# Two hybrid blocks on one core: the input transposed once and used unnormalised by the first four projections, the attention mask written into PSUM by VectorE

## The chip, the cores and the metric

The kernel runs on one core of a Trainium2 chip. The metric is the device time of one execution in microseconds (us). The kernel before takes 1582.7 us, the median of three runs (1582.47 to 1582.87).

## The reference, cut to what matters

One sequence of 512 positions and 1024 features passes through two blocks. Everything is float32. The parts that the change touches:

```
h = concat(16 meta tokens, x)                      # 528 rows are used
n = h * rsqrt(mean(h*h, features) + 1e-6) * norm_mix_w
z = n @ w_in[1024, 7168]                           # q, k, v, glu (2 x 1024), two gates
s = (q * 64**-0.5) @ k.T                           # 8 heads x 2 maps, chunks of 64 positions
p = softmax(where(chunk(key) <= chunk(query), s, -1e30))
o = (p[0] - lam * p[1]) @ v;  y_att = rms(o) * subln_w * 0.2
u = glu[:1024] * sigmoid(glu[1024:]);  u = causal depthwise conv over 31 positions
u = silu(layernorm(u));  m = gate * y_att + gate * (u @ w_conv_out);  h = h + m @ w_out
... feed-forward with a 3 tap convolution, then block 2: an mLSTM, a linear recurrence,
    a 256-of-512 sparse attention with 4 heads, another feed-forward ...
```

The rms norm of a row is one factor per position. A projection of h * norm_mix_w therefore equals the projection of n once each of its columns (positions) is multiplied by that factor.

## The kernel before, in words

Activations lie with features on the 128 partitions: a tile holds 128 features by 528 positions, and eight tiles make the residual (`res`) or the normalised input (`xn`). Products are made with float32r parts. Each operand is split into a rounded part and the rest, and a product is three matmuls (weight high with activation high, weight high with activation low, weight low with activation high). A weight block of 1024 x 128 arrives by DMA as `raw`, ScalarE rounds it into `wh`, VectorE subtracts it into `wl`; three such pairs are buffered. A step (`step`, L566) is the six matmuls of one of the eight feature tiles, a projection (`units`, `one`) is eight steps.

Order is made at build time. `Build` keeps a model clock for TensorE (`pe`), and a model time for VectorE and for ScalarE (`Lane`, L158). Generators (`start`, `tick`) emit side work between the projection's steps when the model says that what they read is ready, and the operations of the 31 tap convolution wait in a list (`bg`) and are emitted one by one while the model's VectorE is no further than 0.3 us ahead of its TensorE. The hardware then runs each engine's instructions strictly in the order emitted. In `tick` the weight feed comes first, the convolution last.

The input phase (`load_x`, L601): five row tiles `xt` arrive by DMA. ScalarE squares them with a sum, the inverse roots are found in two parts (first two tiles, then three), VectorE multiplies the row tiles by the root into `xs`, and TensorE transposes `xs` into PSUM tile by tile (`parts`, `turn`), where ScalarE and VectorE make the two parts of `xn`. The raw tiles `xt` are transposed too, for the residual: four feature tiles into PSUM in `prepare`, the last rows and the four other feature tiles later in `raw`, which `block1_mix` starts. The projections start when `xn[0]` is there.

The list `units1` sets the order of projections in block 1: for each of eight feature tiles a pair of gated-unit projections (`glu`: `e_b` is the tanh half, `e_a` the value half) followed by three head projections (q, k, v, gate of a head in turn), then the remaining heads and gates. `glu(0)` runs its two projections in a skewed manner, as the input arrives. After the last value half the convolution has to run dry (`after_conv`), then `layer_norm` makes `us[0..7]`, and the projection with `w_conv_out` waits for each `us[k]`.

In `attention`, each head computes scores of four blocks of 128 queries. A mask is added by one small bfloat16 matmul per map and block (`ind` by `neg`, L331 to L336, L795 and L815). VectorE finds the row maximum, multiplies it by -0.125, and ScalarE does the exponential with scale 0.125. At the end of a head VectorE scales the four output blocks in one operation. The convolution (`conv_ops`, L753) of one feature tile is two `tensor_scalar`, 29 `scalar_tensor_tensor` that go in turn to two accumulators `a` and `b`, the sum of the two, and an add to `csum`.

Of the kernel before, what the change touches and what calls it, by code (L numbers as in the profile page):

```python
# [9 lines left out]
F32R = mybir.dt.float32r  # L10
# [7 lines left out]
P = 128  # L18
# [144 lines left out]
class Build:  # L163
# [159 lines left out]
    def constants(self):  # L323
        nc, c = self.nc, self.const
        self.ident = c.tile([P, P], F32, name="ident")
        make_identity(nc, self.ident)
        self.identb = c.tile([P, P], BF, name="identb")
        nc.vector.tensor_copy(self.identb, self.ident)
        self.ones = c.tile([P, P], F32, name="ones")
        nc.vector.memset(self.ones, 1.0)  # L330
        self.ind = c.tile([P, P], BF, name="ind")  # L331
        nc.vector.memset(self.ind, 0.0)
        for m in range(2):
            nc.vector.memset(self.ind[64 * m : 64 * m + 1, 0:64], 1.0)
        self.neg = c.tile([P, 64], BF, name="neg")
        nc.vector.memset(self.neg, NEG)  # L336
# [264 lines left out]
    def load_x(self):  # L601
        nc, io, V, S = self.nc, self.io, self.V, self.S
        x, meta = io["x"][0], io["meta_tokens"]
        self.res = [self.resp.tile([P, NT], F32, name=f"res{j}", tag="res") for j in range(KD)]
        self.xn = [None] * KD
        rows = [P, P, P, P, NMETA]
        xt = [self.flat(D) for _ in range(5)]
        xs = [self.flat(D) for _ in range(5)]
        v = self.sm(5, "xv")
        V.memset(v, 1.0)  # L610
        at = (1, 2, 3, 4, 0)
# [3 lines left out]
        for t in range(4):  # L615
# [15 lines left out]
        def turn(src, pt, j):  # L631
            for t in range(5):
                w = rows[t]
                self.tr(pt[:, t * P : t * P + w], src[t][:w, j * P : (j + 1) * P])

        def scale(ts, r, g):
            c = slice(512 * g, 512 * g + 512)
            for i, t in enumerate(ts):
                V.tensor_scalar(xs[t][: rows[t], c], xt[t][: rows[t], c], r[: rows[t], i : i + 1], None, op0=MUL)

        def inverse(lo, n):
            vb = v[:, lo : lo + n]
            yield self.due(vb)
            V.tensor_scalar(vb, vb, 1.0 / D, 1e-6, op0=MUL, op1=ADD)
            return (yield from self.rsqrt_act(vb, n))

        raws = [self.mm_ps(), self.mm_ps()]
        rawv = lambda j: raws[j // 2][:, (j % 2) * 512 : (j % 2) * 512 + 512]

        def square(t):  # L650
            S.activation(xs[t][: rows[t]], xt[t][: rows[t]], AF.Square, accum_out=v[: rows[t], at[t] : at[t] + 1])

        def prepare():

            S.activation(self.sm(1, "yw"), v[:, 0:1], AF.Sqrt)
            self.tr(raws[1][:, 0:8], w8[0:8])
            yield self.due(raws[1])
            V.tensor_copy(wmix, raws[1][:, 0:8])
            square(4)
# [9 lines left out]
            r = yield from inverse(2, 3)  # L669
            scale((1, 2, 3), r, 0)  # L670
            self.wp_max = 1
            for p in range(2):
                self.start(parts(p))
            yield self.due(raws[0])
            for j in range(2):
                S.activation(self.res[j][:, 0:512], rawv(j), AF.Copy)
            yield self.due(xs[3][:, 0:512])
            yield 4.0
            scale((1, 2, 3), r, 1)
            for j in range(2, 4):  # L680
                S.activation(self.res[j][:, 0:512], rawv(j), AF.Copy)

        def parts(p):

            for j in range(p, KD, 2):
                i, pt = yield from self.at_get()
                yield self.due(*[xs[t][: rows[t], j * P : (j + 1) * P] for t in range(5)])
                turn(xs, pt, j)
# [6 lines left out]
                yield self.due(n)  # L695
                self.at_put(i)

        def raw():
            i, pr = yield from self.at_get()
            for j in range(4):  # L700
                self.tr(pr[:, j * NMETA : (j + 1) * NMETA], xt[4][:NMETA, j * P : (j + 1) * P])
            yield self.due(pr)
            for j in range(4):
                S.activation(self.res[j][:, 512:], pr[:, j * NMETA : (j + 1) * NMETA], AF.Copy)
            self.at_put(i)
            for j in range(4, KD):
                yield 2.0
                i, pr = yield from self.at_get()
                turn(xt, pr, j)
                yield self.due(pr)  # L710
                S.activation(self.res[j], pr[:, :NT], AF.Copy)
                self.at_put(i)
# [3 lines left out]
        self.until(lambda: self.xn[0] is not None)  # L716
        return raw

    def one(self, segs, acts, evac):
# [4 lines left out]
        self.units([[(pt[:, o : o + m], m, c) for o, m, c in segs]], acts, evac=lambda u: evac(pt[:, lo : lo + n]))  # L724
# [28 lines left out]
    def conv_ops(self, j, u, a, b, csum):  # L753
        V = self.V
        w = lambda k: self.col("conv_dw_w", k * 8 + j)
        ops = [
            lambda: V.tensor_scalar(a, u[:, 0:NQ], w(0), self.col("conv_dw_b", j), op0=MUL, op1=ADD),
            lambda: V.tensor_scalar(b, u[:, 1 : 1 + NQ], w(1), None, op0=MUL),
        ]
# [10 lines left out]
    def attention(self, tp, h, qk, vs, ctx):  # L770
# [5 lines left out]
        made, used = [], [0]  # L776
        mask = lambda m: (self.ind[64 * m : 64 * m + 64, :], self.neg[64 * m : 64 * m + 64, :])
# [3 lines left out]
        def softmax(i):  # L781
            L = 144 + 128 * i
            q = lambda m: qT[64 * m : 64 * m + 64, 2 + 128 * i : 130 + 128 * i]
            mx, nb, l = self.sm(2, "mx"), self.sm(2, "nb"), self.sm(2, "ll")
            e = self.slot()

            def ex(m, sv):
                S.activation(e[:, m, :L], sv, AF.Exp, bias=nb[:, m : m + 1], scale=0.125, accum_out=l[:, m : m + 1])

            yield self.due(qT)  # L790
            if i < 3:
                i_at, pt = yield from self.at_get()
                for m in range(2):
                    mm(pt[:, 512 * m : 512 * m + L], q(m), k(m, 0, L), True, False)
                for m in range(2):  # L795
                    mm(pt[:, 512 * m + L - 64 : 512 * m + L], *mask(m), False, True)
                    if i == 0:
# [6 lines left out]
                V.tensor_reduce(mx, pair(pt)[:, :, :L], axis=AX.X, op=MAX)  # L804
                V.tensor_scalar(nb, mx, -0.125, None, op0=MUL)
# [1396 lines left out]
```

## Time and profile before

| what | value |
|---|---|
| median of three runs | 1582.7 us |
| the profiled execution's own time | 1582.17 us |
| its span, first to last instruction | 1580.4 us |
| TensorE busy | 1561.0 us, 99% of the span |
| VectorE busy | 1116.5 us, 71% |
| ScalarE busy | 650.8 us, 41% |

The span is the time from the first to the last instruction; the own time is 1.8 us more. A line of the profile's views names an engine (PE is TensorE, PEld its weight loads, DVE is VectorE, ACT is ScalarE), the line of the kernel, the operation, and the tiles written and read; L158 is the helper through which VectorE and ScalarE are called, L314 that of matmuls, L320 that of transposes, so a row is told by its tiles. `act<-u,par,act` is a tap of the long convolution, `at` and `mm` are PSUM tiles.

### The profile page before, as it was taken

The page shows a single profiled execution, that of the slowest core. Times are in us where ns is not written, and L with a number is a line of the kernel's source. Part 1 is how long each engine was busy: PE and PEld are TensorE (multiplying, and loading weights), DVE is VectorE, ACT ScalarE, POOL GpSimd, SP SyncE. Part 2 cuts the span into 40 slices and gives each one's busy share as a digit, 9 for nine tenths or more (in the row PEclk, how much of TensorE's full clock was granted, in tenths as well). Part 3 has the DMA queues.
Part 4 walks back from the last instruction along what each step waited for, and adds up shares of the span by engine and source line. Part 5 has one row for each costly group of instructions (what it writes and reads, how often), then busy time and mean ns, then how long its engine had stood idle before and what let it go on. Part 6 is the DMA issues. An engine that isn't in the chain of part 4 may idle for free.

```text
span 1580.4 us, 25476 instructions
## 1 busy us (share of the span) xinstructions
PE 1561.0 (99%) x10349; PEld 1397.7 (88%) x10349; DVE 1116.5 (71%) x2083; ACT 650.8 (41%) x1166; POOL 26.2 (2%) x89
## 2 busy tenths in 40 slices
PE   7999999999999999999999999999999999999998
PEld 6999999999999999999988877797799888888886
DVE  4989999997864676767743357898868877775224
ACT  5344434445542344434432222635466544444122
POOL 3000000000000000000000000000000000000000
PEclk9999999999999999999999999999999999999999
DMA  4322222222222323333333332231054133333221
GB/s 144 95 64 71 68 81 67 68 67 68 67 61 88 103 86 93 94 94 94 89 89 87 91 100 79 67 108 54 5 144 120 54 93 94 93 94 106 95 93 67
DMA packets 233005, 134.17 MB, mean 85 GB/s; under 512 B 6926, under 2 KB 228241, under 8 KB 232889
## 3 DMA queue, kind: packets, MB, share of 16 engines
q1 hardware_dynamic: 231448, 130.35, 28.3%
q8 instruction: 81, 1.33, 0.3%
q0 software_dynamic: 1136, 1.15, 0.3%
q10 hardware_dynamic: 304, 1.05, 0.2%
q14 instruction: 36, 0.29, 0.1%
HBM read 130.44 MB, written 2.10 MB: 84 GB/s over the span
## 4 chain that ended last, share of the span: by engine, by line
PE 98%; ACT 1%; DVE 1%; DMA 0%; issue 0%; DVEq 0%; ACTq 0%; POOLq 0%
PE mm L314 70%; PE at L314 25%; PE at L320 3%; ACT act L158 0%; DMA act<-in_x_dram 0%; DVE yy L158 0%; DVE act L158 0%; ACT ys L158 0%; DVE yc L158 0%; ACT e L158 0%; ACT wh L158 0%; DVE fx L158 0%; DVE res L158 0%; DVEq L2198 0%; ACT rsy L158 0%
## 5 line engine op out<-in xcount | busy, mean ns | idle before, releaser
L314 PE MATMUL mm<-act,wh 128*128 128x256 f32 (+3 forms) x4720 | 907.6, 306 | 1.2 <-ACT act L158 0.5
L314 PEld LDWEIGHTS mm<-act,wh 128*128 128x128 f32 (+1 forms) x4720 | 692.7, 189 | 48.0 <-issue 9.4
L314 PE MATMUL mm<-act,wl 128*128 128x256 f32 (+4 forms) x2360 | 563.1, 303 | 0.0
L158 DVE TENSOR_TENSOR wl<-raw,wh 128x1024 fp32r<-128x1024 f32 (+2 forms) x235 | 284.4, 1211 | 170.4 <-ACT wh L158 168.1
L158 ACT ACTIVATE wh<-raw 128x1024 fp32r<-128x1024 f32 (+2 forms) x235 | 245.7, 1047 | 376.0 <-PE mm L314 195.4
L314 PEld LDWEIGHTS mm<-act,wl 128*128 128x128 f32 (+1 forms) x2360 | 383.2, 189 | 18.1
L158 DVE SCALAR_TENSOR_TENSOR act<-u,par,act 128x514 f32<-128x514 f32 x232 | 160.4, 748 | 0.0
L314 PE MATMUL at<-act,wh 128*128 128x512 f32 x416 | 130.2, 394 | 0.0
L314 PEld LDWEIGHTS at<-act,wh 128*128 128x128 f32 x416 | 78.0, 188 | 18.2
L314 PE MATMUL at<-wh,act 128*128 128x512 f32 x264 | 85.9, 395 | 0.0
L314 PE MATMUL at<-act,act 128*128 128x256 f32 (+8 forms) x468 | 83.8, 328 | 0.0
L314 PE MATMUL mm<-wh,act 128*128 128x256 f32 (+1 forms) x344 | 83.7, 318 | 0.0
L314 PE MATMUL at<-act,wl 128*128 128x512 f32 x208 | 82.1, 394 | 0.0
L158 DVE TENSOR_TENSOR act<-act,act 128x514 f32<-128x514 f32 (+4 forms) x122 | 69.9, 590 | 6.1 <-ACT act L158 5.5
L158 ACT ACTIVATE act<-mm 128x528 f32<-128x528 f32 (+2 forms) x64 | 35.1, 549 | 91.4 <-PE mm L314 91.2
L314 PEld LDWEIGHTS at<-act,act 128*128 128x128 f32 (+1 forms) x468 | 60.7, 189 | 10.1 <-issue 4.0
L158 DVE SCALAR_TENSOR_TENSOR ft<-fx,par,ft 128x512 f32<-128x512 f32 x88 | 65.8, 749 | 1.6
L158 DVE TENSOR_TENSOR fx<-mm,rB 128x514 f32<-128x514 f32 x44 | 30.5, 694 | 50.2 <-PE mm L314 50.0
L158 ACT ACTIVATE act<-at 128x128 f32<-128x128 f32 (+4 forms) x88 | 34.7, 413 | 73.2 <-PE at L314 56.5
L314 PEld LDWEIGHTS mm<-wh,act 128*128 128x128 f32 x344 | 57.8, 189 | 7.1 <-issue 3.2
L158 DVE SCALAR_TENSOR_TENSOR gy<-gx,par,gy 128x512 f32<-128x512 f32 x84 | 62.6, 748 | 1.5
L314 PEld LDWEIGHTS at<-wh,act 128*128 128x128 f32 x264 | 49.6, 188 | 11.4
(290 smaller groups left out, 1463.0 us busy)
## 6 DMA issues: line engine op xcount, KB each, us to landing
raw<-in_w_in_dram SPq DMA_DIRECT2D x82, 512.0 KB, 3.6
raw<-in_w_up_dram SPq DMA_DIRECT2D x44, 512.0 KB, 3.7
raw<-in_ffn_up_dram SPq DMA_DIRECT2D x44, 512.0 KB, 3.9
raw<-in_ffn_down_dram SPq DMA_DIRECT2D x22, 512.0 KB, 3.2
raw<-in_w_out_dram SPq DMA_DIRECT2D x20, 512.0 KB, 3.7
raw<-in_w_down_dram SPq DMA_DIRECT2D x16, 512.0 KB, 3.5
raw<-in_w_conv_out_dram SPq DMA_DIRECT2D x8, 512.0 KB, 3.8
raw<-in_w_down_dram SPq DMA_DIRECT2D x8, 384.0 KB, 3.3
```

The source lines that it names most:

```text
L158: return f(*a, **k)
L314: self.nc.tensor.matmul(out, lhsT, rhs, start=start, stop=stop)
L320: self.nc.tensor.transpose(out, src, self.ident[p0 : p0 + k, p0 : p0 + k])
```

## The change

The row tiles `xt` are transposed once. VectorE copies each transposed tile from PSUM into `res`. From `res` come the two parts of `xr`, which is h * norm_mix_w without the norm. The first four projections (both halves of `glu(0)`, q and k of head 0) use `xr`, and VectorE multiplies their results by the row of inverse roots `r0`, which is found from all five tiles at once and spread over the partitions by matmuls with ones. Later projections use `xn`, made from `res`, the weight column and `r0`. The mask is a VectorE memset of 64 partitions in PSUM, before the maximum; the two constant tiles are gone. The scale 0.125 goes into q, and the maximum is negated by the reduction itself. In block 2's sparse attention the same is done, and its transposed weights use two fixed half tiles. The convolution starts with a ScalarE operation and uses one accumulator. The four output blocks of a head are scaled by four ScalarE operations.

```diff
 load_x
-            self.loaded(xt[t], 5.0 + 1.55 * t)
+            self.loaded(xt[t], 10.0 if t else 7.0)
...
-            self.loaded(self.raws[i], 11.2 + 1.5 * i)
+            self.loaded(self.raws[i], 10.3 + 1.5 * i)
...
         def prepare():
+            ats = []
+            for _ in range(2):
+                ats.append((yield from self.at_get()))
+            self.wp_max = 1
             for t in range(4):
                 yield self.due(xt[t])
-                square(t)
-                for j in range(4):
-                    self.tr(rawv(j)[:, t * P : (t + 1) * P], xt[t][:, j * P : (j + 1) * P])
+                for j in range(2):
+                    turn(t, ats[j][1], j)
                 if t == 0:
-                    r = yield from inverse(0, 2)
-                    for g in range(2):
-                        scale((4, 0), r, g)
+                    for j in range(2):
+                        turn(4, ats[j][1], j)
+                    square(4)
+                    square(0)
             for p in range(2):
-                self.start(parts(p))
+                self.start(parts(p, *ats[p]))
+            self.start(stats(), 2.0)
...
         def parts(p, i, pt):
             for j in range(p, KD, 2):
+                if j != p:
+                    i, pt = yield from self.at_get()
+                    for t in range(5):
+                        turn(t, pt, j)
                 yield self.due(pt)
                 n = self.slot(F32R)
-                self.split_scaled(n, pt[:, :NT], wmix[:, j : j + 1], NT)
-                self.xn[j] = n
+                V.tensor_copy(self.res[j], pt[:, :NT])
+                yield self.due(self.res[j])
+                self.at_put(i)
+                self.split_scaled(n, self.res[j], wmix[:, j : j + 1], NT)
+                self.xr[j] = n
                 if j == 1:
                     self.wp_max = 3
...
+        def stats():
+            for t in (1, 2, 3):
+                square(t)
+                yield 1.5
+            yield self.due(v)
+            V.tensor_scalar(v, v, 1.0 / D, 1e-6, op0=MUL, op1=ADD)
+            r = yield from self.rsqrt_act(v, 5)
+            yield from self.bcast_cols(r, rows, rB0, True)
+            yield self.due(rB0)
+            self.r0 = rB0
+            tmp = self.slot()
+            for p in range(2):
+                self.start(norm(p, tmp[:, p, :]))
+
+        def norm(p, t):
+            for j in range(p, KD, 2):
+                while self.xr[j] is None:
+                    yield 0.2
+                yield self.due(self.res[j])
+                V.scalar_tensor_tensor(t, self.res[j], wmix[:, j : j + 1], rB0, op0=MUL, op1=MUL)
+                yield self.due(t)
+                n = self.slot(F32R)
+                self.split_sb(n, t, NT)
+                self.xn[j] = n
+                yield 0.5
 conv_ops
-            lambda: V.tensor_scalar(a, u[:, 0:NQ], w(0), self.col("conv_dw_b", j), op0=MUL, op1=ADD),
-            lambda: V.tensor_scalar(b, u[:, 1 : 1 + NQ], w(1), None, op0=MUL),
-        for k in range(2, CK):
-            d = a if k % 2 == 0 else b
-            ops.append(lambda k=k, d=d: V.scalar_tensor_tensor(d, u[:, k : k + NQ], w(k), d, op0=MUL, op1=ADD))
-        ops.append(lambda: V.tensor_tensor(a, a, b, op=ADD))
+        self.S.activation(a, u[:, 0:NQ], AF.Identity, scale=w(0), bias=self.col("conv_dw_b", j))
+        for k in range(1, CK):
+            ops.append(lambda k=k: V.scalar_tensor_tensor(a, u[:, k : k + NQ], w(k), a, op0=MUL, op1=ADD))
 attention
-                for m in range(2):
-                    mm(pt[:, 512 * m + L - 64 : 512 * m + L], *mask(m), False, True)
...
                 yield self.due(pt)
+                V.memset(pair(pt)[0:64, :, L - 64 : L], NEG)
...
-                V.tensor_reduce(mx, pair(pt)[:, :, :L], axis=AX.X, op=MAX)
-                V.tensor_scalar(nb, mx, -0.125, None, op0=MUL)
+                V.tensor_reduce(nb, pair(pt)[:, :, :L], axis=AX.X, op=MAX, negate=True)
...
-                V.tensor_copy(rl0[:, i : i + 1], rl[:, 0:1])
...
-            V.tensor_tensor(o3(1), o3(0), sc[:, :, None].to_broadcast([P, 4, P]), op=MUL)
...
+            for i in range(4):
...
+                S.activation(o_sb[:, 1, b], o_sb[:, 0, b], AF.Copy, scale=sc[:, i : i + 1])
 block1_mix
-            self.start(raw(), 4.0)
...
+                    if s == 0:
+                        self.until(lambda: self.r0 is not None)
+                        V.tensor_tensor(tb, p, self.r0, op=MUL)
...
+                    if s == 0:
+                        V.tensor_tensor(u[:, CK - 1 :], u[:, CK - 1 :], self.r0, op=MUL)
...
+                acts = self.xr if h == 0 and i < 2 else self.xn
```

## Rows read from the trace of the kernel before

**Rows 1.** The page: busy time of TensorE, and the chain by engine.

```profile
PE 1561.0 (99%) x10349; PEld 1397.7 (88%) x10349; DVE 1116.5 (71%) x2083; ACT 650.8 (41%) x1166; POOL 26.2 (2%) x89
...
PE 98%; ACT 1%; DVE 1%; DMA 0%; issue 0%; DVEq 0%; ACTq 0%; POOLq 0%
```

**Rows 2.** Timeline of PE, first 24 us: start, length, work, idle before.

```profile
9.98 1.97 PE L320 MATMUL mm<-ident,act 128*128 128x128 f32 x8 [2.02 <-DMA act<-in_x_dram]
...
17.60 1.25 PE L314 MATMUL mm<-act,wh 128*128 128x264 f32 x4
...
20.40 1.87 PE L320 MATMUL at<-ident,act 128*128 128x128 f32 x10
...
23.12 0.51 PE L314 MATMUL mm<-act,wh 128*128 128x264 f32 x2 [0.29 <-DVE act L158]
```

**Rows 3.** The first weight block: issue and landing (us), then ACT and DVE timelines.

```profile
L526 SPq DMA_DIRECT2D raw<-in_w_in_dram x1: 429/429/429, 2.1 to 2.1; - x1
...
DMA to landing us min/median/max: 9.5/9.5/9.5
...
13.38 1.04 ACT L158 ACTIVATE wh<-raw 128x1024 fp32r<-128x1024 f32 x1
...
15.52 1.21 DVE L158 TENSOR_TENSOR wl<-raw,wh 128x1024 fp32r<-128x1024 f32 x1
```

**Rows 4.** Timeline of PE, 24 to 32 us: transposes between matmuls.

```profile
24.20 0.40 PE L314 MATMUL mm<-act,wl 128*128 128x264 f32 x2
24.44 0.76 PE L320 MATMUL at<-ident,act 128*128 128x128 f32 x5
25.13 0.76 PE L314 MATMUL mm<-act,wh 128*128 128x264 f32 x4
...
31.40 0.42 PE L320 MATMUL at<-ident,act 16*128 16x16 f32 x4
```

**Rows 5.** Matmuls with ones, grouped, 395 to 402 us: count, busy us, mean ns.

```profile
L314 PE MATMUL at<-act,ones 128*128 128x128 f32 x8 | 1.1, 274 | 0.0
```

**Rows 6.** The mask matmuls: all of them, then timeline of PE around two.

```profile
L314 PE MATMUL at<-neg,ind x68: 189/189/200, 78.1 to 1098.8; 64*128 64x64 bf16 x68
...
83.45 0.20 PE L314 MATMUL at<-neg,ind 64*128 64x64 bf16 x2
83.57 0.74 PE L314 MATMUL mm<-act,wh 128*128 128x256 f32 x4
```

**Rows 7.** DVE operations grouped by shape, 0 to 366 us: busy us, mean ns.

```profile
L158 DVE SCALAR_TENSOR_TENSOR act<-u,par,act 128x514 f32<-128x514 f32 x232 | 160.4, 748 | 0.0
...
L158 DVE TENSOR_TENSOR act<-act,act 128x514 f32<-128x514 f32 x14 | 9.7, 693 | 0.3
...
L158 DVE TENSOR_SCALAR act<-u,par 128x514 f32<-128x514 f32 x16 | 7.8, 515 | 0.2
...
L158 DVE TENSOR_TENSOR act<-act,sc 128x512 f32<-128x512 f32 x6 | 4.1, 691 | 0.2
...
L158 DVE COPY rl<-rl 128x1 f32<-128x1 f32 x25 | 3.7, 147 | 0.0
L158 DVE TENSOR_SCALAR nb<-mx 128x2 f32<-128x2 f32 x20 | 3.4, 169 | 0.7
...
L330 DVE MEMSET ones<- 128x128 f32 x1 | 0.2, 165 | 0.0
```

**Rows 8.** Timeline of DVE: taps to two accumulators in turn, and to one.

```profile
49.33 4.07 DVE L158 SCALAR_TENSOR_TENSOR act<-u,par,act 128x514 f32<-128x514 f32 x6
...
1252.09 1.53 DVE L158 SCALAR_TENSOR_TENSOR gy<-gx,par,gy 128x512 f32<-128x512 f32 x2
```

**Rows 9.** Stretches: length, then PE, PEld, DVE busy (operations), ACT, POOL, granted clock.

```profile
39.00:366.00 327.00, 327.00 (x2639) 310.15 (x2638) 301.88 (x603) 132.12 (x330) 0.75 (x6) 1.00 0.25 72
366.00:456.00 90.00, 90.00 (x725) 84.04 (x724) 69.47 (x170) 48.97 (x110) 3.86 (x11) 1.00 0.25 71
```

**Rows 10.** Timelines of DVE (last tap, last `us`) and PE (first use of it).

```profile
364.81 0.75 DVE L158 SCALAR_TENSOR_TENSOR act<-u,par,act 128x514 f32<-128x514 f32 x1
...
454.59 0.69 DVE L158 TENSOR_TENSOR act<-act,act 128x514 fp32r<-128x514 f32 x1 [0.88 <-ACT act L158]
...
461.47 0.72 PE L314 MATMUL mm<-act,wh 128*128 128x256 f32 x4
```

More of the change, by code (lines that the diff above doesn't have):

```diff
@@ L629, in load_x @@
         wmix = self.const.tile([P, 8], F32, name="wmix")
[L631 to L645, printed above, removed]
@@ L685, in parts @@
+                    square(4)
+                    square(0)
+            for p in range(2):
+                self.start(parts(p, *ats[p]))
+            self.start(stats(), 2.0)
+        def parts(p, i, pt):
             for j in range(p, KD, 2):
-                i, pt = yield from self.at_get()
-                yield self.due(*[xs[t][: rows[t], j * P : (j + 1) * P] for t in range(5)])
-                turn(xs, pt, j)
+                if j != p:
+                    i, pt = yield from self.at_get()
+                    for t in range(5):
+                        turn(t, pt, j)
@@ L696, in parts @@
[L696 to L712, printed above, removed]
+        def stats():
[11 more added lines that the diff above has]
+                self.start(norm(p, tmp[:, p, :]))
@@ L717, in load_x, with one @@
-        return raw
-    def one(self, segs, acts, evac):
+        self.until(lambda: self.xr[0] is not None)
+    def one(self, segs, acts, evac, have=None):
         pt = self.mm_ps()
@@ L723, in one @@
         n = sum(s[1] for s in segs)
-        self.units([[(pt[:, o : o + m], m, c) for o, m, c in segs]], acts, evac=lambda u: evac(pt[:, lo : lo + n]))
+        self.units([[(pt[:, o : o + m], m, c) for o, m, c in segs]], acts, have=have,
+                   evac=lambda u: evac(pt[:, lo : lo + n]))
     def lam_col(self):
@@ L775, in attention @@
         qT, kT, vT, sg = qk[:, 0, :], qk[:, 1, :], vs[:, 0, :], vs[:, 1, :]
-        made, used = [], [0]
-        mask = lambda m: (self.ind[64 * m : 64 * m + 64, :], self.neg[64 * m : 64 * m + 64, :])
+        made, used, l0 = [], [0], self.sm(4, "l0", bufs=4)
         k = lambda m, a, b: kT[64 * m : 64 * m + 64, a:b]
@@ L813, in softmax @@
                     mm(pt[:, 248:512], q(m), k(m, 0, 264), True, True)
[L814 to L815 removed]
+                    mm(pt[:, 512:776], q(m), k(m, 264, 528), True, True)
                     yield self.due(pt)
[L817 to L818 removed]
+                    V.memset(pt[0:64, 712:776], NEG)
+                    V.tensor_reduce(nb[:, m : m + 1], pt[:, 248:776], axis=AX.X, op=MAX, negate=True)
                     yield self.due(nb)
@@ L888, in second @@
             yield self.due(ss0)
-            v = self.sm(4, "ssv")
+            v, rl0 = self.sm(4, "ssv"), self.sm(4, "rl0")
+            V.reciprocal(rl0, l0)
             V.tensor_tensor(v, rl0, rl0, op=MUL)
@@ L1136, in e_g @@
                     atts.append(self.attention(tp, h, hold["qk"], hold["vs"], (sx, v16, th16, w8, yav(h), state)))
-                self.one(SEG_ALL if i in (1, 2) else SEG_Q, self.xn, (e_q, e_k, e_v, e_g)[i])
+                acts = self.xr if h == 0 and i < 2 else self.xn
+                self.one(SEG_ALL if i in (1, 2) else SEG_Q, acts, (e_q, e_k, e_v, e_g)[i],
+                         have=lambda k: acts[k] is not None)
             us = [None] * 8
@@ L1750, in sparse @@
                 yield self.due(pt)
-                eT = self.flat(SEQ)
+                while not ets:
+                    yield 0.1
+                eT = ets.pop()
                 S.activation(eT[:, :L], pt[:, :L], AF.Copy)
@@ L2163 @@
     b.plan_weights()
-    raw = b.load_x()
-    b.block1_mix(raw)
+    b.load_x()
+    b.block1_mix()
     b.block1_ffn()
```

119 lines of the change are left out of this document (55 added, 64 removed).

## The prediction

> **What bounds the kernel now.** I read the page first. TensorE is busy 1561.0 of 1580.4 us, and the chain that ended last is TensorE for 98% [rows 1]. So time comes off only where TensorE loses work or waits, and the change costs time only where it makes TensorE wait. I then read the timeline of PE at the start: the reader is to see transposes at 9.98 as the input lands, the first projection matmul at 17.60, ten more transposes at 20.40, and a wait for VectorE at 23.12 [rows 2]. After that TensorE does not stop while VectorE, busy 301.9 of 327 us between 39 and 366, is the next fullest engine [rows 9]. Last I looked for the place where VectorE's work comes due. It is `us[7]`: the last tap ends at 365.6, `us[7]` is done at 455.3, and TensorE first needs it at 461.47 [rows 10]. That is 6.2 us to spare, in a kernel where the change takes work from TensorE and shifts VectorE's.
>
> **The change part by part.** All sums are against the profiled execution's own 1582.17 us; the median of the runs is 0.5 above that, and I take the difference to the median.
>
> Start. The raw projections do not wait for the norm, but the first weight block still lands at 2.1 + 9.5 = 11.6. Rounding it takes 1.04 and its low part 1.21 [rows 3], so `wl` ends near 13.9. In the model's times the weight feed emits that `wl` (due 11.3) before the copies of tiles 0 and 1 (due 11.6), and VectorE runs in order, so copy 0 waits until 13.9 although its transposes end near 11. A copy of 128x528 from PSUM to SBUF by VectorE is not in the trace; it lies between the 0.515 of a `tensor_scalar` and the 0.693 of a `tensor_tensor` [rows 7]. I take 0.69, the nearer one in that it gives no credit for a single source; the other end would save 8 x 0.18 = 1.4 us of VectorE. Copies 0 and 1 end at 14.6 and 15.3. They free the two PSUM slots, and the transposes of tiles 2 and 3 are emitted ahead of the first step: ten of them took 1.87 [rows 2], the second five not before 15.3, so the first matmul comes near 17.4 instead of 17.60. Gained: 0.2 there, 1.87 for the ten transposes no longer at 20.40, and 0.3 for the wait at 23.12 [rows 2]. `stats`, with its squares, root and matmuls with ones, ends before the first projection does, and the norm multiplications wait for it, so `xr` is not slowed by them.
>
> Transposes of the raw input. `raw` had four groups of five and one of four small ones; a group of five occupies TensorE for 0.76, the small one for 0.42 [rows 4]. They stood between full-rate matmuls, nothing hides them, and all of it is gone: 3.46. Added are five matmuls with ones, which the profile shows as ten instructions: eight took 1.1 [rows 5], so 1.35.
>
> Mask. A mask matmul lasts 189 ns, but two that run together delay the next matmul by 0.12 (83.45 to 83.57) [rows 6]. A head has two alone in its first block, a pair in the second and in the third, and two alone in the last: six slots, 0.72. Eight heads give 5.8, the four in block 2 (two pairs) 0.24, together 6.0. Bounds: 0, if the handover to the next matmul takes as long without them, and 68 x 0.19 = 12.9. I take the gap to the next matmul, since that is what the row shows directly. The memset that replaces them is not in the trace for PSUM; the nearest is 128x128 in SBUF at 0.165, against the 0.169 of the operation removed with it (`nb`) [rows 7], so VectorE is even. The score tile waits longer for release by one such operation, and nothing but side work queues for it.
>
> Edits at nothing: ScalarE takes on a first tap and four small scalings; it is busy 132 of 327 us in this stretch [rows 9] and has room. In block 2 the removed `nb` shortens each sparse step by 0.15 and two fixed half tiles may hold one up; I leave both at zero, within 1 us either way.
>
> TensorE's sum: 0.2 + 1.87 + 0.3 + 3.46 - 1.35 + 6.0 = 10.5 us less.
>
> VectorE up to the last tap. Added: normalising eight tiles, 8 x (0.75 + 0.69) = 11.5, and four multiplications by `r0`, 2.8; less 2.2, by which the first projection ends earlier. The convolution: one accumulator means that each tap waits for the last. Six taps that alternate take 4.07, which is 0.664 each after the first's 0.75; two where the second needs the first take 1.53, so 0.78 [rows 8]. About two thirds of the 240 taps stand directly behind another: 160 x 0.116 = 18.5. One more tap in each of eight tiles adds 6.0, the removed `tensor_scalar` save 16 x 0.515 = 8.2 and the removed sums 8 x 0.69 = 5.5: together 10.8 more, for fewer operations. In the heads the 25 small copies save 3.7 and the six scalings 4.1, and a reciprocal in each adds about 1.0 by the same small copies [rows 7]: 6.8 less. Net 16.1 us more.
>
> Whether that reaches TensorE depends on how much of VectorE's idle time it can take: 25.1 us up to 366, and 20.5 us from there to 456 [rows 9]. Much of it is VectorE waiting for TensorE or ScalarE, and an engine that runs later waits less. With a share a of the 45.6 us used up, `us[7]` is ready at 455.3 + 16.1 - 45.6a. TensorE, 9.9 us ahead by then (all but block 2's masks and part of the last head's), wants it at 461.5 - 9.9 = 451.6. The wait is 19.8 - 45.6a. I take a = 0.4, since the two stretches already have VectorE at 92% and 77%: a wait of 1.6. The weights are split some 10 us ahead of use (three buffers), so a lag of VectorE up to that does not stop the projections before.
>
> One rule of the Trainium skill weighs on this. The page VectorE: DVE Perf Modes, section The DRAIN you can't avoid, says that consecutive operations pay the pipeline flush in any case and that a semaphore after each costs nothing extra. By it the single accumulator would be free, the ledger would be 2.4 less than before instead of 16.1 more, and no wait would be left. The two rows on the taps differ by 0.116 us an operation and speak against it.
>
> Forecast: 1582.7 - 10.5 + 1.6 = 1573.8 us.
>
> **The rivals.**
>
> VectorE becomes the bound. If its idle time cannot be used because the waits recur, `us[7]` is late by the whole 19.8 and the time is 1582.7 - 10.5 + 19.8 = 1592.0, slower. It decides at a = 0.20, where the wait eats all that TensorE gains. For it: only 6.2 us to spare, VectorE at 92%, and each tap dearer. Against: VectorE's waits are mostly for the very engine that now runs ahead. Below a = 0.13 the result is slower by over 0.2% (chance 0.13); from 0.13 to 0.27 it is 1579.5 to 1585.9, no difference (chance 0.12).
>
> The copies come before the first `wl` on VectorE. The model's times differ by 0.3 us only. Then copy 0 ends near 11.7, ScalarE's rounding of tile 0 follows that of the weights, and the first matmul comes near 15.4, 2.0 earlier; with no wait at `us[7]` the time is 1582.7 - 10.5 - 2.0 = 1570.2. Chance 0.12.
>
> The change does not do what it says for the mask: TensorE's handover costs the same without it and the 6.0 stay. TensorE is then less far ahead and the wait vanishes: 1582.7 - 4.5 = 1578.2. For it: the gap of 0.12 is shorter than the matmul's own 0.19. Chance 0.12.
>
> Dependent taps cost no more than alternating ones in this mix, because other work always falls between: the 18.5 go, no wait is left, 1572.2. Chance 0.05, since the rows show long runs of taps. This is the time that the Trainium skill's rule cited above would give.
>
> **How the numbers follow.** The forecast has 0.46; its own range is 1571 to 1579, by a from 0.28 up. A difference under 0.2%, 3.2 us, cannot be told from none. Faster by more than that: 0.46 + 0.12 + 0.12 + 0.05 = 0.75; within: 0.12; slower: 0.13. The range for 8 in 10 is 1569 to 1584.5: its low end takes in the earlier start and a dearer mask, its high end half-way into the wait; left out are most of the slower case and masks at their upper bound.
>
> **What would show it.** In the profile after: no mask matmuls and the gap to the next matmul 0.12 shorter; the first matmul near 17.4 with `wl` ahead of the first copy; the end of the first projection about 2 us earlier; taps in a row at 0.78; VectorE over 95% busy from 40 to 360; `us[7]` near 453 and TensorE waiting for it by 1 to 2 us. A PE idle of over 10 us ahead of the `w_conv_out` projection would make the prediction wrong, as would stalls of the projections for `wl` before it.

## The result: slower, because VectorE delivers late

The changed kernel takes 1607.84 us (1606.28 to 1608.3) against 1582.59 for the kernel before: a ratio of 1.0154, 95% interval 1.0141 to 1.0166. I forecast 1573.8, faster. The page of the changed kernel, first its busy time and then the chain of work that ended last by engine:

```profile
PE 1565.8 (98%) x10249; PEld 1398.0 (87%) x10251; DVE 1130.5 (70%) x2037; ACT 667.9 (42%) x1200; POOL 25.0 (2%) x89
...
PE 92%; DVE 5%; ACT 1%; DMA 1%; issue 1%; SPq 0%; DVEq 0%; ACTq 0%
```

The chain was TensorE for 98% [rows 1]; now it is 92%, and VectorE stands in it for 5% of the span. What TensorE waited for over the whole span (engine, line, what it waited for: us in total, times, longest):

```profile
PE mm L314 <- DVE u L158: 7.1, 2, 4.9
PE mm L314 <- ACT act L158: 6.0, 5, 3.1
PE at L320 <- DMA act<-in_x_dram: 5.5, 3, 3.1
PE at L320 <- DVE res L158: 4.3, 1, 4.3
PE mm L314 <- DVE act L158: 3.0, 7, 1.0
```

The rows for the DMA and for `res` lie ahead of the first projection matmul, where TensorE waited before too. The others are new, but for one wait of 0.5 us for `act` from ScalarE and one of 0.3 us for `act` from VectorE. Stretches of the changed kernel, with the columns of [rows 9]:

```profile
39.00:366.00 327.00, 317.47 (x2499) 298.79 (x2497) 292.46 (x540) 142.32 (x351) 1.02 (x6) 0.99 0.25 71
366.00:456.00 90.00, 90.00 (x718) 83.32 (x717) 73.83 (x175) 47.56 (x117) 2.98 (x11) 1.00 0.22 61
...
456.00:482.00 26.00, 17.82 (x73) 14.21 (x72) 22.85 (x49) 13.48 (x24) 0.00 (x0) 0.61 0.14 39
```

TensorE stood still 9.5 us in the first stretch and 8.2 in the last, which is the start of the `w_conv_out` projection, at a mean granted clock of 0.61. And VectorE, which I had expected to be over 95% busy up to 366, was *less* busy than before: 292.5 of 327 instead of 301.9.

Now VectorE's own timeline in the changed kernel: its first tap, the taps ahead of the second late `u`, its last taps, and the last two halves of layer-norm outputs.

```profile
56.51 0.75 DVE L158 SCALAR_TENSOR_TENSOR act<-u,par,act 128x514 f32<-128x514 f32 x1
...
263.18 7.07 DVE L158 SCALAR_TENSOR_TENSOR act<-u,par,act 128x514 f32<-128x514 f32 x9
270.28 0.70 DVE L158 TENSOR_TENSOR act<-act,act 128x514 f32<-128x514 f32 x1
270.89 0.70 DVE L158 SCALAR_TENSOR_TENSOR u<-act,mm 128x528 f32<-128x528 f32 x1
...
404.75 3.13 DVE L158 SCALAR_TENSOR_TENSOR act<-u,par,act 128x514 f32<-128x514 f32 x4
...
478.34 1.30 DVE L158 TENSOR_TENSOR act<-act,act 128x514 fp32r<-128x514 f32 x2
```

The first tap comes at 56.5 (before: 40.6) and the last ends at 407.9 (before: 365.6 [rows 10]). Nine taps in a row take 7.07, which is 0.787 from start to start. `u` of tile 6 stands behind them, and with it a PSUM tile that TensorE needs: that is its wait of 4.95 at 266.7. The last row holds the seventh and eighth layer-norm outputs, done at 479.0 and 479.6. In the kernel before, the seventh was done at 446.7:

```profile
446.00 0.69 DVE L158 TENSOR_TENSOR act<-act,act 128x514 fp32r<-128x514 f32 x1
```

TensorE there, in the changed kernel:

```profile
457.91 0.40 PE L314 MATMUL mm<-act,wl 128*128 128x256 f32 x2
460.23 1.20 PE L320 MATMUL at<-ident,act 128*128 128x128 f32 x4 [1.92 <-ACT act L158]
464.58 0.79 PE L314 MATMUL mm<-act,wh 128*128 128x256 f32 x2 [3.14 <-ACT act L158]
466.33 0.80 PE L314 MATMUL mm<-act,wh 128*128 128x256 f32 x2 [0.96 <-DVE act L158]
...
476.33 1.56 PE L314 MATMUL mm<-act,wh 128*128 128x256 f32 x4
...
478.36 1.53 PE L314 MATMUL mm<-act,wh 128*128 128x256 f32 x4
...
483.20 0.63 PE L314 MATMUL mm<-act,wh 128*128 128x256 f32 x4
```

The projection makes output tiles 0 and 1 together: one step of six matmuls for each of the first seven outputs and tile 0, then the same seven for tile 1, then the eighth output for both. The first seven steps ran from 447.08 to 454.1 before, and the seventh of them started at 453.12:

```profile
453.12 0.72 PE L314 MATMUL mm<-act,wh 128*128 128x256 f32 x4
```

Now the seventh starts at 478.36, and each step takes 1.8 us or more, the pace at which VectorE makes the outputs. Four matmuls take 1.56 there and 0.63 after it. The granted clock of that stretch, in the columns of [rows 9], is the lower of its two levels (0.50, that is 1.2 of 2.4 GHz):

```profile
461.70:482.20 20.50, 14.51 (x52) 11.90 (x53) 17.67 (x29) 9.52 (x16) 0.00 (x0) 0.50 0.09 26
```

Summed from the trace, from the first projection matmul to the first of the FFN: TensorE waits 17.3 us instead of 0.3, its matmuls take about 11 us more where the clock is low, and its work has become about 5.5 us less. With 0.4 us at the start and 1.4 in the rest of the program that is the 24.3 us between the spans.

### The profile page after: what moved, and what is told of

Read it like the earlier page. It is cut to its first block, busy times and chain, and to the rows that moved or that the text cites. A ratio compares the mean times of both kernels' runs of the same rounds, so it can differ in the third digit from the quotient of the medians.

```text
span 1604.7 us, 25275 instructions
## 1 busy us (share of the span) xinstructions
PE 1565.8 (98%) x10249; PEld 1398.0 (87%) x10251; DVE 1130.5 (70%) x2037; ACT 667.9 (42%) x1200; POOL 25.0 (2%) x89
## 4 chain that ended last, share of the span: by engine, by line
PE 92%; DVE 5%; ACT 1%; DMA 1%; issue 1%; SPq 0%; DVEq 0%; ACTq 0%
PE mm L314 66%; PE at L314 24%; DVE act L158 4%; PE at L320 2%; ACT act L158 1%; DVE wl L158 1%; DMA raw<-in_w_in_dram 1%; DVE yy L158 0%; ACT wh L158 0%; DVE u L158 0%; DVE rsa L158 0%; DVE rsy L158 0%; DVE nb L158 0%; ACT ys L158 0%; DVE yc L158 0%
## 5 line engine op out<-in xcount | busy, mean ns | idle before, releaser
L314 PEld LDWEIGHTS mm<-act,wh 128*128 128x128 f32 (+1 forms) x4720 | 698.1, 191 | 70.2 <-issue 13.7
L158 DVE SCALAR_TENSOR_TENSOR act<-u,par,act 128x514 f32<-128x514 f32 x240 | 180.5, 752 | 5.4
L314 PEld LDWEIGHTS at<-act,wh 128*128 128x128 f32 x416 | 78.1, 188 | 18.2
L314 PE MATMUL at<-act,act 128*128 128x256 f32 (+9 forms) x468 | 83.5, 329 | 0.8 <-ACT act L158 0.7
L158 DVE TENSOR_TENSOR act<-act,act 128x514 f32<-128x514 f32 (+5 forms) x122 | 70.0, 591 | 4.3 <-ACT act L158 3.6
L158 ACT ACTIVATE act<-at 128x128 f32<-128x128 f32 (+7 forms) x89 | 35.0, 415 | 79.7 <-PE at L314 62.2
L158 ACT ACTIVATE act<-act 128x128 f32<-128x128 f32 (+10 forms) x95 | 51.7, 556 | 26.7 <-DVE act L158 21.8
```

What stands on the lines that cost most here:

```text
L158: return f(*a, **k)
L314: self.nc.tensor.matmul(out, lhsT, rhs, start=start, stop=stop)
```

## The experiments

In the table, "input" is the new `load_x` with the raw projections, "conv" the convolution with one accumulator, "heads" the masks in PSUM, the shorter heads and the sparse step of block 2. "Last tap" is its end; "seventh" is when the low half of the seventh layer-norm output is done, "step 7" when TensorE starts on it. All in us, from each run's profiled execution, whose own time lies up to 4.8 us from the median; "time" is the median.

```
kernel                     last tap  seventh  step 7  time    ratio to before, 95%
before                      365.6    446.7    453.1   1582.6
input only                  382.6    460.1    460.5   1588.8  1.0037 (1.0024-1.0050)
conv only                   400.3    470.1    469.5   1596.4  1.0090 (1.0075-1.0105)
heads only                  361.8    448.2    451.4   1584.2  1.0001 (0.9990-1.0011)
input + heads               379.0    457.3    456.6   1585.7  1.0019 (1.0009-1.0028)
conv + heads                398.2    469.4    468.8   1599.2  1.0091 (1.0070-1.0112)
input + conv                416.0    481.6    480.9   1613.3  1.0182 (1.0157-1.0207)
all (the change)            407.9    479.0    478.4   1607.8  1.0154 (1.0141-1.0166)
before, taps reordered      399.6    472.3    471.6   1598.6  1.0099 (1.0075-1.0123)
  in tiles 0 to 3 only      382.1    464.4    465.2   1593.1  1.0065 (1.0050-1.0080)
  in tiles 4 to 7 only      383.0    460.8    461.5   1588.6  1.0046 (1.0026-1.0066)
all, three u                423.0    479.2    478.5   1608.5  1.0156 (1.0136-1.0175)
all, wait filled            407.8    480.2    479.5   1607.9  1.0154 (1.0132-1.0175)
input+heads, ScalarE taps   373.4    455.2    455.9   1581.3  0.9986 (0.9975-0.9997)
heads, ScalarE taps         351.7    433.0    454.0   1579.5  0.9968 (0.9956-0.9979)
input+heads, taps and norm  372.0    455.3    455.9   1581.9  0.9985 (0.9973-0.9997)
```

Theory 1 says that VectorE is short of time and that the moment at which it delivers the layer norm sets the end. Its rivals blame one part: the late start of the taps (A), the single accumulator (B), single waits or the clock.

Time less "step 7" lies between 1125 and 1133 in every row: to within 4 us either way, the moment of that step carries the time of all these kernels. Smaller differences between rows must be read elsewhere.

**One part alone.** Input only, against the kernel before:

```
-        self.split_scaled(n, pt[:, :NT], wmix[:, j : j + 1], NT)     # pt: turned scaled rows
+        V.tensor_copy(self.res[j], pt[:, :NT])                        # pt: turned raw rows
+        self.split_scaled(n, self.res[j], wmix[:, j : j + 1], NT)     # raw; the norm's product follows
```

> Only the input part of the change: input turned raw, copied by VectorE, four projections raw, norm by features on VectorE; convolution, masks and heads as before. Theory 1 (VectorE is short of time, and no single part overruns what it has to spare): taps start some 16 us later than before, TensorE saves about 4, little of it is waited for again: 1577 to 1586. Rival A (the late start of the taps alone is what costs the time): nearly the whole loss, 1600 to 1610. Rival B (the single accumulator alone costs it): a plain gain of 4, 1578.

1588.75. TensorE reaches the first head 2.1 us earlier and is rid of the raw transposes, but taps begin at 57.3 instead of 40.6, and the delay stays: the last tap is 17.0 later. Theory 1 misses by 3, and neither rival holds.

Convolution only:

```
-            lambda: V.tensor_scalar(a, u[:, 0:NQ], w(0), self.col("conv_dw_b", j), op0=MUL, op1=ADD),
-            lambda: V.tensor_scalar(b, u[:, 1 : 1 + NQ], w(1), None, op0=MUL),
+        self.S.activation(a, u[:, 0:NQ], AF.Identity, scale=w(0), bias=self.col("conv_dw_b", j))
...
-            d = a if k % 2 == 0 else b
-        ops.append(lambda: V.tensor_tensor(a, a, b, op=ADD))
```

> Only the convolution of the change: first tap on ScalarE, 30 taps to one accumulator, no sum. Theory 1: VectorE has 11 to 13 us more to do, conv 7 ends 11 to 15 us later than 365.6, the last layer-norm output comes at most 5 us later, TensorE waits 0 to 5: 1582 to 1588. Rival A: no change, 1582.6. Rival B: 1600 to 1610.

1596.41, the largest single share, far outside the range of Theory 1 and short of that of rival B: the last tap moved by 34.7 us, not 11 to 15. Here TensorE's waits sum to 6.1 us, and its matmuls take some 7 to 8.5 us more at the lower clock.

Masks and heads only:

```
-                    mm(pt[:, 512 * m + L - 64 : 512 * m + L], *mask(m), False, True)
+                V.memset(pair(pt)[0:64, :, L - 64 : L], NEG)
-                V.tensor_reduce(mx, pair(pt)[:, :, :L], axis=AX.X, op=MAX)
-                V.tensor_scalar(nb, mx, -0.125, None, op0=MUL)
+                V.tensor_reduce(nb, pair(pt)[:, :, :L], axis=AX.X, op=MAX, negate=True)
```

> Only the masks written into PSUM, the heads with fewer VectorE operations, and block 2's sparse step. Every theory has VectorE with less to do. By my sum for TensorE it gains 6.0 and the time is 1576.6; if the handover after a score matmul costs as much without the mask, 1582; from the trace of the changed kernel, where score matmuls took 2.8 us more than before, 1579.

1584.16, no difference, and nearest to the second figure. TensorE's work up to the FFN is 3.15 us less, and it waits 2.9 us more, at 433.4 for ScalarE and at 461.4 for VectorE.

**One part undone.** Each of these takes the part's lines back to those of before.

> The changed kernel with the convolution of before (two accumulators in turn, all on VectorE). Theory 1: VectorE has 12 us less to do than in the changed kernel; the waits for u and for the last layer-norm output shrink from 17 us to 0 to 6 and with them the stretches at the lower clock: 1575 to 1588. Rival A (late start): still 1598 to 1606. Rival B (single accumulator): 1574.

1585.66: without the single accumulator 22 of the 25 us are gone.

> The changed kernel with the input part of before (norm ahead of the first projection, eight tiles scaled on ScalarE and VectorE from PSUM). VectorE gets through 16 us of taps earlier than in the changed kernel. Theory 1, by the delays of the seventh layer-norm output (convolution part +23, heads +1): its wait is that of the convolution part alone, less the 3 us of masks: 1592 to 1597. If the input part is what costs the time: 1580 to 1585.

1599.18, 2 us above Theory 1's range: the input's share is 9.

> The changed kernel with the masks, heads and sparse step of before. Theory 1: the end is set by VectorE's work up to the layer norm, so TensorE's 3 us of masks are not missed, and the heads' VectorE work, some 4 to 7 us more, is: 1607 to 1616. If TensorE's own work counted, 1611.

1613.33, so the part that gains nothing alone seems to save 5 here, though the two intervals just overlap: VectorE has 4.5 us less to do in the heads.

The delays of the seventh output nearly add up (13.4 for the input and 23.4 for the convolution; together 34.9). The times do not (6, 14; together 30): the kernel before has 6.4 us between the output and its use, and they are spent once.

**The order of the taps.** The kernel before, with the same instructions:

```
-        for k in range(2, CK):
+        for k in [*range(2, CK, 2), *range(3, CK, 2)]:
             d = a if k % 2 == 0 else b
```

> The kernel before with one thing changed: a tile's even taps are emitted first and its odd taps after them, so each tap needs the sum of the tap before it. Same instructions, same number, same operands. If a dependent tap costs 0.122 us more (0.787 against 0.665 between starts in the traces), some 150 taps cost VectorE 18 us, the last tap ends near 384 instead of 365.6, and TensorE waits ahead of the convolution's output projection as with the convolution part alone: 1590 to 1602. If dependence costs nothing (the Trainium skill, VectorE: DVE Perf Modes, section The DRAIN you can't avoid), 1582.6.

1598.57: +16 us from an order. Its taps as a group, six in a row, its last tap, and its seventh and eighth outputs:

```profile
L158 DVE SCALAR_TENSOR_TENSOR act<-u,par,act 128x514 f32<-128x514 f32 x232 | 173.8, 752 | 4.8
...
49.43 4.70 DVE L158 SCALAR_TENSOR_TENSOR act<-u,par,act 128x514 f32<-128x514 f32 x6
...
398.82 0.75 DVE L158 SCALAR_TENSOR_TENSOR act<-u,par,act 128x514 f32<-128x514 f32 x1
...
471.59 1.30 DVE L158 TENSOR_TENSOR act<-act,act 128x514 fp32r<-128x514 f32 x2
```

Six taps take 4.70 where alternating ones took 4.07 [rows 8]; one tap is reported at 752 ns and was at 748, so the mean of a group hides it, and only the distance between starts shows it. Summed from start to start, the convolution costs 184.0 us of VectorE instead of 166.0. By the Trainium skill (VectorE: DVE Perf Modes, section The DRAIN you can't avoid), read as in the prediction, it would have cost nothing. What that section measured is a row of copies with and without semaphores, not operations that need each other's result; for these the measurement decides against the rule.

But 18.0 us of work put the last tap off by 34.0. More than the order of the taps has changed. The build's model takes a result as ready 0.13 us after its operation ends, for a reader on VectorE too (`LAT` in `Model`). So the build, too, holds a tap that needs the one ahead of it for dearer, and emits other operations ahead of the later taps. VectorE from the start to the end of the last tap, in the kernel before and in the reordered one (columns of [rows 9]):

```profile
0.00:365.56 365.56, 354.93 (x2804) 333.71 (x2805) 319.25 (x649) 153.87 (x369) 15.77 (x44) 1.00 0.27 80
...
0.00:399.57 399.57, 388.94 (x3074) 366.34 (x3075) 345.03 (x687) 168.91 (x405) 15.98 (x44) 1.00 0.27 80
```

There are 687 operations instead of 649. Of the 34.0 us some 18 are the taps', some 14 are those 38 other operations, and the rest is idle time. So the 16 us are the price of the order in this build. What dearer taps alone would cost, with every other operation left in its place, no run shows. The convolution part alone moves operations in the same way: 39 more of the others stand between its first tap and its last.

Two runs with half of the dearer taps each ask why the last tap moves so far; the loop over `k` is the reordered one where `j < 4` or where `j > 3`:

> The kernel before, even taps first and odd taps after them in tiles 0 to 3 only: 9 us of dearer taps, early. If taps run in the time that weights and heads leave over (54% of VectorE from tile 2 on) and VectorE has some 10 us to spare between tiles 1 and 2 (last tap 107.3, next tile's first 117.4), the last tap comes 6 to 10 us later than 365.6 and the seventh layer-norm output 4 to 8 later than 446.7, about what it has to spare: 1582 to 1586. If each us of VectorE's work simply comes once at the end, the last tap comes 9 later as in the other half: both runs the same, 1584 to 1587.

> The same in tiles 4 to 7 only: 9 us of dearer taps, late, with no spare time behind them. If taps run in the time left over, 9 us become 9 / 0.54 = 17 at the last tap (382) and some 13 at the seventh output (460), 6 to 7 more than it has to spare: 1587 to 1592. If each us comes once: last tap 375, output 456, 1583 to 1587.

1593.06 and 1588.61. In each the convolution costs 9.2 us more, and 663 operations end with the last tap instead of 649. Late, the last tap ends at 383.0, 17.4 later; the row of the last two taps, and of the sixth and seventh outputs:

```profile
381.46 1.53 DVE L158 SCALAR_TENSOR_TENSOR act<-u,par,act 128x514 f32<-128x514 f32 x2
...
459.50 1.29 DVE L158 TENSOR_TENSOR act<-act,act 128x514 fp32r<-128x514 f32 x2
```

That is what the leftover-time theory gave (382 and 460), and not the other (375 and 456). From tile 2 on the convolution, its sums included, has 54% of VectorE's time in the kernel before (132.9 of 247.3 us, summed from the trace); the build places the splits of weights and the heads at TensorE's pace in any case, so each us more of taps meets up to 0.86 us more of those before it is done (6 us for 9.2 here). Early, both theories missed: the last tap comes 16.5 later, so there are no 10 us to spare between tiles 1 and 2, and the seventh output comes at 464.4, later than with the late half. Why, no run shows.

**Waits that do not count.** The changed kernel with a third buffer for `u`:

```
-                    while len(self.bg) > CK:
+                    while len(self.bg) > 2 * CK:
-                    u = tp.tile([P, CK - 1 + NT], F32, name=self.nm("u"), tag="u")
+                    u = tp.tile([P, CK - 1 + NT], F32, name=self.nm("u"), tag="u", bufs=3)
```

> The changed kernel with three buffers for u instead of two, so that the next u needn't wait for the taps of the one before the last. The two waits for u (2.1 and 5.0 us at 224.8 and 266.7) go, with the lower clock behind the second. Theory 1 (VectorE's total time up to the layer norm sets the end): TensorE reaches the output projection some 9 us earlier and waits that much longer there: 1603 to 1610, no gain. Rival C (these waits are losses of their own): 1597 to 1600.

1608.5, as Theory 1 had it. Its waits (the same view as for the changed kernel):

```profile
PE mm L314 <- ACT act L158: 8.4, 5, 5.6
...
PE at L314 <- DVE cs L158: 5.1, 1, 5.1
...
PE at L314 <- DVE act L158: 3.1, 1, 3.1
```

No wait for `u` is left. TensorE ends the projection before it 12 us earlier (446.4 instead of 458.3), but starts on the first output at 465.3 instead of 464.6. VectorE's row with the seventh and eighth outputs shows why: the seventh is done at 479.2 instead of 479.0.

```profile
478.48 1.30 DVE L158 TENSOR_TENSOR act<-act,act 128x514 fp32r<-128x514 f32 x2
```

Its last tap ends 15.1 us later than in the changed kernel (423.0), and the seventh output comes at the same time. So the last tap by itself does not set that output: other work of VectorE, which stood behind the taps, has gone ahead of them.

The changed kernel with matmuls that nothing reads:

```
+            i_f, pf = self.at_now()
+            for _ in range(30):
+                self.mm(pf[:, 0:128], self.ident, self.ident)
+            self.at_put(i_f)
             self.pairs(SEG_H, us, e_c, have=lambda k: us[k] is not None)
```

> The changed kernel with 30 matmuls of the identity (6.4 us at the full clock) ahead of the convolution's output projection, where TensorE stands idle for 7.6 us in five waits; nothing reads their result. If the clock falls because TensorE was idle, it stays at 1.00, the projection's matmuls are 0.12 apart instead of 0.21, and 4 to 8 us come back although work is added: 1600 to 1604. If the lower clock has another cause, the time rises by up to 6: 1608 to 1614.

1607.85, no change. The clock holds, as the first reading had it, and yet nothing comes back. Its TensorE there:

```profile
458.10 6.86 PE L314 MATMUL at<-ident 128*128 128x128 f32 x60
464.80 0.60 PE L320 MATMUL at<-ident,act 128*128 128x128 f32 x4
466.70 0.51 PE L314 MATMUL mm<-act,wh 128*128 128x256 f32 x2 [1.30 <-ACT act L158]
...
470.32 1.57 PE L314 MATMUL mm<-act,wh 128*128 128x256 f32 x4
...
479.55 1.53 PE L314 MATMUL mm<-act,wh 128*128 128x256 f32 x4
```

While TensorE is kept busy the clock holds: four transposes take 0.60 where they took 1.20 after the idle 1.92. From 468.4 it is low again, after waits of 1.3 and 0.3. The low stretch is 13.7 us long instead of 20.5. But the projection's seventh step starts at 479.5 instead of 478.4: a faster TensorE only waits longer for the next output. So that part of the lower clock was time in which it would have waited anyway. For the rest it is argued from the steps, which go at the pace of the outputs.

**Towards a better kernel.** Two accumulators, the first tap of each on ScalarE:

```
-            lambda: V.tensor_scalar(a, u[:, 0:NQ], w(0), self.col("conv_dw_b", j), op0=MUL, op1=ADD),
-            lambda: V.tensor_scalar(b, u[:, 1 : 1 + NQ], w(1), None, op0=MUL),
+        self.S.activation(a, u[:, 0:NQ], AF.Identity, scale=w(0), bias=self.col("conv_dw_b", j))
+        self.S.activation(b, u[:, 1 : 1 + NQ], AF.Copy, scale=w(1))
```

> Input, mask and head parts of the change; the convolution keeps two accumulators, but ScalarE makes the first tap of both (16 operations of VectorE at 0.4 go). Theory 1: VectorE ends the convolution 6 us earlier than without that, the wait of 3.4 us ahead of the output projection and the lower clock behind it go: 1578 to 1581, faster than both kernels. Rival: the wait there has its cause in the layer norm's own chain and not in the end of the convolution: 1585.

1581.33, 0.3 above the range: 4 us better than without, and a shade faster than before.

> The kernel before with the masks and heads of the change, two accumulators in turn, and the first tap of both on ScalarE. VectorE has 6 us less to do in the convolution than with the masks and heads alone. Theory 1: the two waits there, 1.2 and 2.0 us, shrink, and the 3.2 us of TensorE's masks come through: 1579 to 1582. Rival: those waits hang on ScalarE in the heads, and more work on ScalarE makes them longer: 1584 to 1587.

1579.5, ratio 0.9968 (0.9956 to 0.9979), the best version and faster than both kernels. The seventh output comes 21 us ahead of its use. TensorE waits 0.3 us between its first projection matmul and the FFN, yet loses time: in one stretch the clock falls although it is busy throughout.

```profile
436.00:446.00 10.00, 10.00 (x55) 7.70 (x53) 6.22 (x20) 4.47 (x11) 0.00 (x0) 0.75 0.20 54
```

Ahead of the fall stand 16 small matmuls (16 rows to 2 columns):

```profile
438.48 1.90 PE L314 MATMUL at<-act,xaT 16*2 16x128 f32 x16
440.31 0.74 PE L314 MATMUL mm<-act,wh 128*128 128x256 f32 x4
440.89 0.58 PE L314 MATMUL mm<-act,wl 128*128 128x256 f32 x2
441.27 1.06 PE L314 MATMUL mm<-act,wh 128*128 128x256 f32 x4
```

The kernel before has the same 16 at 430.2, not right behind a row of score matmuls, and there the clock stays at 1.00. The cause of the fall is open.

Last, input, heads and ScalarE taps, with the layer norm's eight scalings on ScalarE too:

```
-                V.tensor_scalar(x, x, half[:, j : j + 1], half[:, 8 + j : 9 + j], op0=MUL, op1=ADD)
                 yield self.due(x)
+                S.activation(x, x, AF.Identity, scale=half[:, j : j + 1], bias=half[:, 8 + j : 9 + j])
```

> The version with input, masks and heads and the first taps on ScalarE, and with the eight scalings of the layer norm on ScalarE too. Theory 1: in the burst ahead of the output projection VectorE gives one output each 1.8 us; without the scaling each takes 0.5 less, and the 2.1 us of waits there go: 1578 to 1580. Rival: the longer way over ScalarE makes each output later: 1582 to 1585.

1581.93, no better than without: ahead of the projection TensorE waits 2.7 us instead of 2.1. Theory 1 missed, the rival about held.

## Why the prediction was wrong

**TensorE, 10.5 us less.** Measured, about 5.5 between the first projection matmul and the FFN. The input began as forecast: head 0 begins 2.05 us earlier (36.61), and `wl` goes ahead of the first copy, though the first matmul comes at 17.99 instead of 17.4. But its terms add up to 4.5 (0.2 + 1.87 + 0.3 + 3.46 - 1.35), and 5.5 less 3.15 for the masks leaves about 2.3, less the 0.4 lost at the start. The forecast also had no waits for the late norm; TensorE waits 2.4 us in five waits at 53 to 58, where it first needs `xn`. The masks gave about half of the 6.0. I took the 0.12 between a pair of mask matmuls and the next matmul as what the mask costs. The row to read was that of the score matmuls without a mask behind them. From the first score matmul to the next projection matmul, in the kernel before:

```profile
82.88 0.73 PE L314 MATMUL at<-act 64*128 64x272 f32 x4
```

and in the changed one:

```profile
82.43 0.73 PE L314 MATMUL at<-act 64*128 64x272 f32 x4
83.09 0.74 PE L314 MATMUL mm<-act,wh 128*128 128x256 f32 x4
```

0.69 with the mask (to 83.57 [rows 6]), 0.66 without. Over all, 5.9 us of masks go and the score matmuls take 2.8 us longer to hand over: 3.15 instead of 6.0 in block 1.

**VectorE, 16.1 us more.** Each term was near, but their sum was not. Dependent taps: 18.5 forecast, 18.0 measured by themselves. The whole convolution: 10.8 forecast, about 13. The heads: 6.8 less forecast, 4.5 less measured. The start: 12.1 forecast (14.3 less the 2.2 of an earlier end), and the first tap comes 15.9 later. Together that is some 24 instead of 16.1. Up to the seventh output VectorE is busy 388.5 us instead of 367.1 (from 39 us on).

**The step that failed is a = 0.4**, that VectorE's idle time would take up part of it, 18.2 us. It took up none: `us[7]`, forecast for 453, came at 479.6, 24.4 later than before, which is all of those 24. Idle time up to the seventh output went from 40.6 to 51.5. Some 5 us of the rise are the gaps between dependent taps themselves, which the profile counts as idle (151 pairs by 0.787 - 0.752). The rest is not room to spare, since the waits behind it recur: for TensorE 15.2 us before and 11.8 after, for ScalarE 16.2 and 23.4. Behind the number was also a wrong picture, that a us of work moves the end by a us or less. The build fixes the order of VectorE's instructions, and the taps have what the weights and the heads leave; the runs with half of the taps show 9.2 us becoming 17 at the last tap and 14 to 18 at the seventh output.

**Which output binds.** I watched the eighth (6.2 us to spare). The first seven are taken one after the other ahead of it and arrive at VectorE's pace; the seventh, with 6.4 to spare before, sets the end. The eighth still has 6.4 us to spare in the changed kernel. By it the loss would have been 24.4 - 6.2 = 18.2; the seventh came 32.3 later, which less 6.4 is 25.9, and TensorE's seventh step came 25.3 later. So the spare time was near, but it belonged to the wrong output.

**"A lag of VectorE up to 10 us does not stop the projections"** failed too: `u` holds a PSUM tile, and its operation stands behind the taps of the tile before the last. The run with three `u` shows that without these 7.1 us the loss is the same.

**The rival** "VectorE becomes the bound" was right in its place and mechanism, that the waits recur, at a chance of 0.13. It was too small: it has `us[7]` at 471.4 and the time at 1592.0, against 479.6 and 1607.8.

What stays open: how much of the loss comes from the chip's slower taps in a fixed order, and how much from the other operations that the build then puts ahead of them; the share of each foreground operation in the stretching, which was worked out from the 54% and not tried one by one; and of the 1.4 us in the rest of the program no cause was looked for.

## What to carry to other kernels

Count work added to a busy in-order engine by what it delays: where a build places background work in the time that foreground work leaves, divide by the share it gets (here each us of taps put the last tap off by nearly two, and the seventh output by 1.4 to 1.9). When an edit changes what such a build believes of an operation, compare the emitted orders too, because more may have moved than the edit says. Read the cost of an operation from start to start in the mix that it will run in, since neither the count of operations nor the mean duration of a group showed that one accumulator is dearer than two. And when TensorE waits for another engine, look for the last delivery that binds before pricing single stalls or a lower clock: taking away two stalls, and a third of a stretch at the lower clock, moved nothing.

## What was not expected of the hardware

A VectorE tap whose input is the result of the tap ahead of it starts 0.787 us after it, against 0.665 in alternation, at durations of 0.752 and 0.748. TensorE's granted clock fell to a mean of 0.75 over 10 us in which it never stood idle, after 64-row score matmuls and 16 matmuls of 16 rows to 2 columns; the kernel before has the same 16 with the clock at 1.00. In the changed kernel it fell in an idle time of 5.0 us (at 270.6) and, at 461.7, just inside one of 3.1 that follows one of 1.9. It held at 1.00 there, until 468.4, when 60 matmul records filled these idle times.
